# A two-layer trunk with experts: rows fetched and returned by indirect DMA in place of one-hot products, and a conv LayerNorm queued behind the gates

## The chip, the cores and the metric

The kernel runs on one core of a Trainium2 chip. The metric is the device time of one execution in microseconds. Engines are named as in the profile: PE is TensorE (PEld its weight loads), DVE is VectorE, ACT is ScalarE, POOL is GpSimd, SP is SyncE, whose queue issues the transfers of the weights.

## What is computed

256 tokens of 1024 channels go through two layers. Each layer has a mixer (a conv module beside four heads of a gated delta rule, with one output projection) and a feed-forward part, each followed by a LayerNorm. The feed-forward part is dense in layer 0 and in layer 1 a choice of two experts of eight per token. The reference, cut to what the change touches:

```python
def conformer_conv(h_val, h_gate, dw_w, dw_b, ln_g, ln_b):
    h = h_val * jax.nn.sigmoid(h_gate)
    h = causal_depthwise_conv(h, dw_w) + dw_b        # 31 taps, 512 channels
    return jax.nn.silu(layer_norm(h, ln_g, ln_b))

def gated_deltanet(...):
    ...
    o = o * lax.rsqrt(jnp.mean(o * o, -1, keepdims=True) + RMS_EPS) * on_g
    o = o * jax.nn.silu(heads(z))

def hybrid_mixer(...):
    return jnp.concatenate([y_conv, y_dn], axis=-1) @ w_out

def moe_swiglu(x, router_w, w_gate, w_up, w_down):   # 8 experts of width 3584
    top_v, top_i = lax.top_k(x @ router_w, TOP_K)    # TOP_K = 2
    gates = jax.nn.softmax(top_v, axis=-1)
    combine = jnp.sum(jax.nn.one_hot(top_i, N_EXPERTS) * gates[..., None], axis=-2)
    for e in range(N_EXPERTS):
        y = y + combine[..., e:e + 1] * swiglu(x, w_gate[e], w_up[e], w_down[e])
```

## The kernel before

**Stages.** Mixer 0, the dense feed-forward part, mixer 1, the router, the experts and a last LayerNorm run one after the other. All weights come from memory in transfers of 1 MB on SP's queue (`load_w`, L152) into 14 buffers, `raw` and `raw2`.

**Products.** Where fp32 precision is wanted from three fast products, a weight half (128x1024) is split into `whi` (a copy in fp32r on ACT, L160) and `wlo` (the rest, a subtraction on DVE, L161). `prod3` (L205 to L207) then makes three products of them: with whi, with wlo, and whi with the low part of the other operand. Four buffers hold each of whi and wlo.

**Experts.** Each expert takes up to 128 tokens and runs seven steps, one per 512 columns of its width (8 x 7 = 56 steps; experts with more tokens are finished by code behind a branch that is not entered). A step has `gateup` (mg and mu, four loads), the transposes of the hidden values (`turn`, L878) and `down` (md, two loads), which runs one step later and adds to two PSUM banks `y`. The order in the program is gateup of a step, then down of the step before; between the two halves of a gateup comes `turn`.

**In and out of an expert.** `onehot(e)` compares each token's slot number with a row of 0 to 127 (L817): pm is a 256x128 one-hot matrix. `dispatch(e)`, called in step 5 of the expert before, multiplies the tokens xs with pm (16 fp32 products, L850), which gathers and transposes in one; ACT and DVE split the result into the pair `xe` (L853, L854). `combine(e)`, called after the last down of an expert, transposes pm (L823) and casts it (L825), splits y into a pair `ysl` (ACT L829, DVE L830), multiplies back to token rows (eight products, L834) and adds each of four pieces, times the gate of its token (comb), to the sum macc (L835 on DVE).

**Mixers.** The conv's 31 taps are spread: POOL and ACT take 11 or 12 of them, DVE the others (`scalar_tensor_tensor`, L640), in blocks of 128 channels, c = 0 to 3; cv is the sum (L642). The conv's LayerNorm starts with transposes of cv on PE (L650), followed by statistics and scaling on DVE (L653), transposes back (L656), swish on ACT (L657) and a split into the pair yTh, yTl (L659, L660). The delta rule ends with `gate_out(tb, po)` for the two halves of the tokens, tb = 0 and 1 (gate 0 and gate 1 in what follows): squares on ACT (L565), a sum `oss` (L566) and an rsqrt of small steps on DVE (L196 to L201), the gated output o (L571) on DVE, four transposes on PE (L572), and a copy yF (L574). The output projection has products of yF with raw weights (L673) and, after these, `prod3` products with yTh and yTl.

**What sets the order.** Each engine runs its own list of instructions. A scheduler ahead of the program places them, by the data that each needs and by a cost of its own; `tc.issue_after(x)` puts what is issued within it behind the instruction x. So a line's place in the code doesn't tell its place on an engine.

Of the kernel before, what the change touches and what calls it, by code (L numbers as in the profile page):

```python
# [7 lines left out]
F32 = mybir.dt.float32  # L8
# [21 lines left out]
ORDER = (('k', 'log', 'v', 'kk', 'q', 'c0', 'inv', 'c1'), ('k', 'log', 'v', 'kk', 'inv', 'q', 'c0', 'c1'))  # L30
GROUPS = {"c0": (0, 1), "c1": (2, 3), "k": (4, 5), "q": (6, 7), "v": (8, 9)}
# [14 lines left out]
def tile_hybrid_trunk(ctx: ExitStack, tc: tile.TileContext, A: dict, out: bass.AP, stop=None):  # L46
# [259 lines left out]
    def mixer(l):  # L306
        with ExitStack() as late:
# [253 lines left out]
            def gate_out(tb, po):  # L561
                oss = mx.tile([P, NH], F32, name="oss", bufs=2)
                oq = mx.tile([P, NH, P], F32, name="oq", tag="dec", bufs=2)
                for h in range(NH):
                    act.activation(oq[:, h], po[:, h], AF.Square, accum_out=oss[:, h:h + 1])  # L565
                dve.scalar_tensor_tensor(oss, oss, 1.0 / P, ssq[:, tb], op0=OP.mult, op1=OP.add)  # L566
                fac = rsqrt(oss, NH, "4")
                o = mx.tile([P, NH, P], F32, name="o", tag="dec", bufs=2)
                pt = psum.tile([P, NH, P], F32, name="sm")
                for h in range(NH):  # L570
                    dve.scalar_tensor_tensor(o[:, h], po[:, h], fac[:, h:h + 1], zg[:, tb, h], op0=OP.mult, op1=OP.mult)  # L571
                    pe.transpose(pt[:, h], o[:, h], ident)  # L572
                dst = (slice(None), slice(None), slice(tb * P, (tb + 1) * P))
                act.activation(yF[dst], pt, AF.Copy)  # L574

# [38 lines left out]
            gate_out(0, po0)  # L614
# [4 lines left out]
            gate_out(1, po1)  # L619
# [4 lines left out]
            for half in range(2):  # L624
# [10 lines left out]
                for m in range(2):  # L635
                    c = 2 * half + m
                    dve.tensor_scalar(ca[:, m], hp[:, c, 0:T], dwh[:, l, c * CW:c * CW + 1], sm_[:, S_DWB + c:S_DWB + c + 1],
                                      op0=OP.mult, op1=OP.add)
                    for j in range(1, CW - NP):
                        dve.scalar_tensor_tensor(ca[:, m], hp[:, c, j:j + T], dwh[:, l, c * CW + j:c * CW + j + 1], ca[:, m],  # L640
                                                 op0=OP.mult, op1=OP.add)
# [108 lines left out]
    def moe(l):  # L750
        with tc.tile_pool(name="moe", bufs=1) as ex:
# [58 lines left out]

            def onehot(e, base):
                pm = ex.tile([P, 2, P], F32, name="pmx", tag="ysl") if base else ex.tile([P, 2, P], F32, name="pm", bufs=2)
# [7 lines left out]
            def combine(e, pm, py, tag="sm"):  # L820
# [5 lines left out]
                ysl = ex.tile([P, 2, D], F32R, name="ysl")  # L826
                for n in range(2):
                    ns = slice(n * 512, (n + 1) * 512)
                    act.activation(ysl[:, 0, ns], py[n], AF.Copy)  # L829
                    dve.tensor_tensor(ysl[:, 1, ns], py[n], ysl[:, 0, ns].bitcast(F32), op=OP.subtract)  # L830
                    for tb in range(2):
                        pc = psum.tile([P, 512], F32, name=tag)
                        for i in range(2):
                            pe.matmul(pc, pmT[:, tb], ysl[:, i, ns], start=(i == 0), stop=(i == 1))  # L834
# [5 lines left out]
            def dispatch(e):  # L840
                pm = onehot(e, 0) if e else pm0
# [51 lines left out]
            disp, ys = {0: dispatch(0)}, {}  # L893
# [7 lines left out]
            def do_down():  # L901
# [4 lines left out]
                if j == NJ - 1:  # L906
# [150 lines left out]
```

## Time and profile before

| What | Value |
|---|---|
| three runs | 1561.82 to 1564.14 us, median 1562.19 |
| the profiled execution | 1562.18 us, of which its span 1560.4 |
| mean granted clock of PE over the span | 0.989 |
| mixer 0; dense part; mixer 1; router | 0 to 170; 170 to 405; 405 to 528; 528 to 546 us |
| experts; last LayerNorm and output | 546 to 1541; 1541 to 1560.4 us |
| PE busy, experts' stage | 452.99 us of the first 454, 539.54 of the other 541 |
| DVE busy, the same | 413.89 and 477.44 |
| 336 loads of expert weights | 1 MB each |

A page of the profile shows one execution on the core. The views used below are the page itself, a table of stretches (the busy time of each engine in a stretch of the span), groups of like instructions, the chain of waits (followed back from the last instruction, at each step to what released it), the sums of waits by what was waited for, and the timeline of one or all engines. In a row of the timeline the idle time before the instruction, and what ended it, stand in brackets. An operation with `x16` in the program can stand with more pieces in the trace.

### The profile page before, as it was taken

To read this page: it belongs to the slowest core of one execution; us is meant where nothing else is said; L and a number is where in the kernel's file an instruction comes from. 1 tells how busy PE (TensorE), PEld (TensorE's weight loads), DVE (VectorE), ACT (ScalarE), POOL (GpSimd) and SP (SyncE) were. 2 spreads that over 40 slices of the span, in tenths; PEclk is the share of its full clock that TensorE was granted. 3 is DMA by queue.
4 is the path that set the end of the run, shared out by engine and by line. 5 is a ranking of instruction groups with operands and counts; after the bars stand their busy time and mean duration, and the time that the engine had idled before them with its cause. 6 is when DMAs were issued, how large, how long until landed. Compare 5 with 4: busy or idle time off the path is not lost.

```text
span 1560.4 us, 20825 instructions
## 1 busy us (share of the span) xinstructions
PE 1512.6 (97%) x7750; PEld 1254.7 (80%) x7750; DVE 1269.1 (81%) x1775; ACT 991.8 (64%) x1267; POOL 94.1 (6%) x80
## 2 busy tenths in 40 slices
PE   8998999999998999999999999999999999999995
PEld 7884899998885778888888888877887887887884
DVE  5987544447978589899899898889888889889887
ACT  3364244443255288778778777777777777777773
POOL 0252000000144000000000000000000000000000
PEclk9999999999999899999999999999999999999998
DMA  8322555545222789999999989999999999999960
GB/s 354 109 81 101 183 179 186 189 163 189 78 85 85 320 329 377 347 353 368 357 340 375 356 330 367 357 351 339 371 346 344 361 341 339 378 343 331 368 234 29
DMA packets 60731, 430.44 MB, mean 276 GB/s; under 512 B 6736, under 2 KB 7120, under 8 KB 9296
## 3 DMA queue, kind: packets, MB, share of 16 engines
q1 hardware_dynamic: 60624, 429.06, 74.0%
q8 instruction: 62, 1.02, 0.3%
q14 instruction: 45, 0.37, 0.1%
HBM read 427.98 MB, written 1.05 MB: 275 GB/s over the span
## 4 chain that ended last, share of the span: by engine, by line
PE 60%; DVE 4%; issue 1%; ACT 0%; DVEq 0%; ACTq 0%
PE gu L206 13%; PE gu L207 12%; PE gu L205 12%; PE y L206 6%; PE y L207 6%; PE y L205 6%; DVE wlo L161 2%; PE sm L850 2%; PE sm L878 1%; DVE macc L835 1%; PE sm L834 1%; ACT whi L160 0%; DVE lny L249 0%; DVE ln_sto L177 0%; DVE lny L252 0%
## 5 line engine op out<-in xcount | busy, mean ns | idle before, releaser
L161 DVE TENSOR_TENSOR wlo<-raw,whi 128x1024 fp32r<-128x1024 f32 x753 | 889.5, 1221 | 162.1 <-ACT whi L160 148.2
L160 ACT ACTIVATE whi<-raw 128x1024 fp32r<-128x1024 f32 x753 | 775.8, 1057 | 193.7 <-PE gu L207 78.4
L206 PE MATMUL gu<-wlo,xe 128*128 128x512 f32 x892 | 352.9, 396 | 1.9 <-DVE wlo L161 1.3
L205 PE MATMUL gu<-whi,xe 128*128 128x512 f32 x892 | 351.6, 395 | 0.0
L207 PE MATMUL gu<-whi,xe 128*128 128x512 f32 x892 | 348.1, 390 | 0.0
L206 PEld LDWEIGHTS gu<-wlo,xe 128*128 128x128 f32 x892 | 167.6, 188 | 44.1 <-DVE wlo L161 12.3
L205 PEld LDWEIGHTS gu<-whi,xe 128*128 128x128 f32 x892 | 167.5, 188 | 36.5 <-ACT whi L160 1.9
L207 PEld LDWEIGHTS gu<-whi,xe 128*128 128x128 f32 x892 | 167.6, 188 | 33.6
L205 PE MATMUL gu<-xTh,whi 128*128 128x256 f32 x320 | 90.9, 284 | 0.0
L207 PE MATMUL gu<-xTh,wlo 128*128 128x256 f32 x320 | 90.6, 283 | 0.0
L206 PE MATMUL gu<-xTl,whi 128*128 128x256 f32 x320 | 90.5, 283 | 0.0
L640 DVE SCALAR_TENSOR_TENSOR ca<-hp,small,ca 128x256 f32<-128x256 f32 x148 | 72.3, 488 | 3.9
L213 PE MATMUL mm<-xT,raw 128*128 128x256 f32 x240 | 56.8, 390 | 8.4 <-DMA raw<-win 7.0
L206 PEld LDWEIGHTS gu<-xTl,whi 128*128 128x128 f32 x320 | 61.4, 192 | 0.6 <-issue 0.2
L205 PEld LDWEIGHTS gu<-xTh,whi 128*128 128x128 f32 x320 | 61.4, 192 | 0.6 <-issue 0.2
L207 PEld LDWEIGHTS gu<-xTh,wlo 128*128 128x128 f32 x320 | 61.4, 192 | 0.0
L213 PEld LDWEIGHTS mm<-xT,raw 128*128 128x128 f32 x240 | 45.8, 197 | 14.7 <-issue 6.9
L871 ACT ACTIVATE h<-gu 128x512 f32<-128x512 f32 x56 | 33.5, 599 | 37.0 <-PE gu L207 36.8
L634 POOL TENSOR_TENSOR cp<-cp,pr 128x512 f32<-128x512 f32 x42 | 53.6, 1275 | 56.1 <-ACT pr L632 54.2
L632 ACT ACTIVATE pr<-hp,small 128x256 f32<-128x256 f32 x84 | 39.2, 505 | 10.8 <-POOL cp L634 10.8
L872 DVE TENSOR_TENSOR h<-h,gu 128x512 f32<-128x512 f32 x56 | 38.3, 683 | 4.3 <-PE gu L207 3.1
L213 PE MATMUL mm<-xF,raw 128*128 128x256 f32 x176 | 40.5, 380 | 1.2 <-ACT whi L160 1.2
(766 smaller groups left out, 2233.1 us busy)
## 6 DMA issues: line engine op xcount, KB each, us to landing
raw<-mu SPq DMA_DIRECT2D x112, 1024.0 KB, 6.9
raw<-mg SPq DMA_DIRECT2D x112, 1024.0 KB, 6.8
raw<-md SPq DMA_DIRECT2D x112, 1024.0 KB, 6.8
raw<-win SPq DMA_DIRECT2D x23, 1024.0 KB, 5.8
raw<-fgu SPq DMA_DIRECT2D x22, 1024.0 KB, 4.9
raw<-fdn SPq DMA_DIRECT2D x11, 1024.0 KB, 5.0
raw<-wout SPq DMA_DIRECT2D x8, 1024.0 KB, 5.0
xT<-xt SPq DMA_DIRECT2D x2, 512.0 KB, 5.7
```

What stands on the lines that cost most here:

```text
L160: act.activation(hi, src, AF.Copy)
L161: eng.tensor_tensor(low, src, hi.bitcast(F32), op=OP.subtract)
L205: pe.matmul(ps, ah, bh, start=start, stop=False, skip_group_check=True)
L206: pe.matmul(ps, ah, bl, start=False, stop=False, skip_group_check=True)
L207: pe.matmul(ps, al, bh, start=False, stop=stop, skip_group_check=True)
L213: pe.matmul(ps, a, b, start=start, stop=stop, skip_group_check=True)
L632: act.activation(pr[:, m], hp[:, c, j:j + T], AF.Copy, scale=dwh[:, l, c * CW + j:c * CW + j + 1])
L634: pool.tensor_tensor(cp[:, cs], cp[:, cs], pr, op=OP.add)
L640: dve.scalar_tensor_tensor(ca[:, m], hp[:, c, j:j + T], dwh[:, l, c * CW + j:c * CW + j + 1], ca[:, m], op0=OP.mult, op1=OP.add)
L850: pe.matmul(pt[:, k], xs[:, tb, (hf * 4 + k) * P:(hf * 4 + k + 1) * P], pm[:, tb], start=(tb == 0 and k == 0), stop=(tb == 1), skip_group_ ...
L871: act.activation(h, pg, AF.Silu)
L872: dve.tensor_tensor(h, h, pu, op=OP.mult)
```

## The change

**Experts.** Before expert 1 is needed, the tokens xs are written to memory (`xrows`, 256 rows), and `number_rows` makes a list of token numbers and, for each token, the row numbers of its two experts' outputs (that of a row of zeros, where the output is expert 7's). `fetch(e + 1)`, in step 1 of expert e, makes pm as before, multiplies it with the column of token numbers (two products with one column each), casts the result to integers `xi` and has POOL fetch the 128 rows by an indirect DMA (512 KB) into `xg`. `dispatch` transposes xg in eight blocks. `put_away` copies y of experts 0 to 6 to `yst` on ACT and writes it from POOL to the memory `yrows` (512 KB). Expert 7 still has its combine. In its steps 1 to 4 `recall` fetches 128 rows of outputs each, first and second choice of both halves of the tokens, and `collect` adds them to macc, each times its gate, in steps 3 to 6.

**Mixers.** The last 12 of DVE's taps in block c = 3 are held: six behind gate 0's last o, six behind gate 1's. The transposes of cv (L650) wait behind gate 1's last transpose.

```diff
-                    dve.scalar_tensor_tensor(o[:, h], po[:, h], fac[:, h:h + 1], zg[:, tb, h], op0=OP.mult, op1=OP.mult)
-                    pe.transpose(pt[:, h], o[:, h], ident)
+                    d = dve.scalar_tensor_tensor(o[:, h], po[:, h], fac[:, h:h + 1], zg[:, tb, h], op0=OP.mult, op1=OP.mult)
+                    t = pe.transpose(pt[:, h], o[:, h], ident)
...
-            gate_out(0, po0)
+            gated = [gate_out(0, po0)]
...
-            gate_out(1, po1)
+            gated.append(gate_out(1, po1))
...
+                        hold_back = ExitStack()
+                        if c == CT - 1 and j >= CW - NP - 2 * HELD:
+                            hold_back.enter_context(tc.issue_after(gated[j >= CW - NP - HELD][0]))
+                        with hold_back:
+                            dve.scalar_tensor_tensor(ca[:, m], hp[:, c, j:j + T], dwh[:, l, c * CW + j:c * CW + j + 1], ca[:, m],
+                                                     op0=OP.mult, op1=OP.add)
...
-                for c in range(CT):
-                    pe.transpose(pt[:, c], cv[:, c, ts], ident)
+                with tc.issue_after(gated[1][1]):
+                    for c in range(CT):
+                        pe.transpose(pt[:, c], cv[:, c, ts], ident)
...
+            def number_rows():
+                for tb in range(2):
+                    pool.dma_start(xrows[tb * P:(tb + 1) * P], xs[:, tb])
...
+            def fetch(e):
+
+                pm = onehot(e, 0)
+                pi = psum.tile([P, 1], F32, name="sm")
+                for tb in range(2):
+                    pe.matmul(pi, pm[:, tb], tok[:, tb:tb + 1], start=(tb == 0), stop=(tb == 1))
+                xi = ex.tile([P, 1], I32, name="xi", bufs=2)
+                dve.tensor_copy(xi, pi)
+                xg = row4("xg")
+                pool.indirect_dma_start(xg, None, xrows[:, :], bass.IndirectOffsetOnAxis(ap=xi[:, 0:1], axis=0))
+                return pm, xg
+
+            def put_away(e, py):
+                yst = row4("yst")
+                for n in range(2):
+                    act.activation(yst[:, n * 512:(n + 1) * 512], py[n], AF.Copy)
+                pool.dma_start(yrows[e * P:(e + 1) * P], yst)
+
+            def recall(i):
+                yg = row4("yg")
+                pool.indirect_dma_start(yg, None, yrows[:, :], bass.IndirectOffsetOnAxis(ap=yi[:, i % 2, i // 2:i // 2 + 1], axis=0))
+                return yg
+
+            def collect(i):
+                tb, yg = i // 2, recalled[i]
+                dve.scalar_tensor_tensor(acc[:, tb], yg, gt[:, i % 2, tb:tb + 1], acc[:, tb], op0=OP.mult, op1=OP.add)
...
             def dispatch(e):
-                pm = onehot(e, 0) if e else pm0
+                pm, xg = fetched.pop(e) if e else (pm0, None)
...
-                    for tb in range(2) if e else ():
-                        for k in range(4):
-                            pe.matmul(pt[:, k], xs[:, tb, (hf * 4 + k) * P:(hf * 4 + k + 1) * P], pm[:, tb],
-                                      start=(tb == 0 and k == 0), stop=(tb == 1), skip_group_check=True)
+                    for k in range(4) if e else ():
+                        pe.transpose(pt[:, k], xg[:, (hf * 4 + k) * P:(hf * 4 + k + 1) * P], ident)
...
+                if j == NJ - 1 and e < NE - 1:
+                    put_away(e, ys[e])
+                elif j == NJ - 1:
                     combine(e, disp[e][0], ys[e])
...
+                if (e, j) == (0, 1):
+                    number_rows()
+                if j == 1 and e + 1 < NE:
+                    fetched[e + 1] = fetch(e + 1)
+                if e == NE - 1:
+                    if j > 2:
+                        collect(j - 3)
+                    if 1 <= j <= 4:
+                        recalled.append(recall(j - 1))
```

Where the scheduler puts this on the engines, by the order of the two programs:

PE, the dispatch for expert 5 within a step of expert 4. `sm` is a PSUM tile, gu and y the products of gateup and down. Before, the first of its five pieces:

```order
L205 MATMUL gu<-whi,xe 128x512
L850 MATMUL sm<-pm,xs 128x128 x3
L206 MATMUL gu<-wlo,xe 128x512
L207 MATMUL gu<-whi,xe 128x512
L205 MATMUL gu<-whi,xe 128x512
```

After (line numbers are those of the changed file):

```order
L206 MATMUL gu<-whi,xe 128x512
L923 MATMUL sm<-keep,xg 128x128 x6
L207 MATMUL gu<-wlo,xe 128x512
L208 MATMUL gu<-whi,xe 128x512
L206 MATMUL gu<-whi,xe 128x512
```

The 16 products, in pieces of 3, 2, 3, 2 and 6, become eight transposes, in pieces of 6 and 2.

DVE, in the combine of expert 5, before:

```order
L161 TENSOR_TENSOR wlo<-raw_11199,whi 128x1024
L161 TENSOR_TENSOR wlo<-raw_11221,whi 128x1024 x2
L161 TENSOR_TENSOR wlo<-raw_11271,whi 128x1024 x2
L830 TENSOR_TENSOR ysl<-y,ysl 128x512 x2
L835 SCALAR_TENSOR_TENSOR macc<-sm,comb,macc 128x512 x2
L161 TENSOR_TENSOR wlo<-raw,whi 128x1024
L835 SCALAR_TENSOR_TENSOR macc<-sm,comb,macc 128x512 x2
L161 TENSOR_TENSOR wlo<-raw,whi 128x1024 x2
L882 TENSOR_TENSOR hp__11320<-sm,hp__11320 128x512
```

After, DVE has nothing of an expert's output until expert 7; there the four additions stand among the splits like this (yg are the rows fetched back):

```order
L162 TENSOR_TENSOR wlo<-raw,whi 128x1024 x4
L883 SCALAR_TENSOR_TENSOR macc<-yg,gt,macc 128x1024
L162 TENSOR_TENSOR wlo<-raw,whi 128x1024 x2
L883 SCALAR_TENSOR_TENSOR macc<-yg,gt,macc 128x1024
L162 TENSOR_TENSOR wlo<-raw,whi 128x1024
L944 TENSOR_TENSOR h<-h,gu 128x512
L162 TENSOR_TENSOR wlo<-raw,whi 128x1024 x3
L954 TENSOR_TENSOR hp__12407<-sm,hp__12407 128x512
L162 TENSOR_TENSOR wlo<-raw,whi 128x1024 x2
L883 SCALAR_TENSOR_TENSOR macc<-yg,gt,macc 128x1024
L162 TENSOR_TENSOR wlo<-raw,whi 128x1024 x2
L883 SCALAR_TENSOR_TENSOR macc<-yg,gt,macc 128x1024
```

Two output splits and four additions in a row per expert have gone; four additions of twice the width stand in two of expert 7's steps.

DVE, gate 0 in mixer 0, before (rs are the steps of rsqrt):

```order
L199 TENSOR_TENSOR rs_t_987<-rs_y_986 128x4
L640 SCALAR_TENSOR_TENSOR ca<-hp,small,ca 128x256
L200 SCALAR_TENSOR_TENSOR rs_t_987<-rs_t_987,oss 128x4
L640 SCALAR_TENSOR_TENSOR ca<-hp,small,ca 128x256
L201 SCALAR_TENSOR_TENSOR rs_y_986<-rs_t_987,rs_y_986 128x4
L642 TENSOR_TENSOR cv<-ca,cp 128x512
L199 TENSOR_TENSOR rs_t_987<-rs_y_986 128x4
L200 SCALAR_TENSOR_TENSOR rs_t_987<-rs_t_987,oss 128x4
L201 SCALAR_TENSOR_TENSOR rs_y_986<-rs_t_987,rs_y_986 128x4
L571 SCALAR_TENSOR_TENSOR o<-sm,rs_y_986,zg 128x128 x4
```

After:

```order
L200 TENSOR_TENSOR rs_t_987<-rs_y_986 128x4
L201 SCALAR_TENSOR_TENSOR rs_t_987<-rs_t_987,oss 128x4
L202 SCALAR_TENSOR_TENSOR rs_y_986<-rs_t_987,rs_y_986 128x4
L572 SCALAR_TENSOR_TENSOR o<-sm,rs_y_986,zg 128x128 x4
L647 SCALAR_TENSOR_TENSOR ca<-hp,small,ca 128x256 x5
L567 SCALAR_TENSOR_TENSOR oss<-oss,ssq 128x4
L647 SCALAR_TENSOR_TENSOR ca<-hp,small,ca 128x256
L197 TENSOR_SCALAR rs_t_1027<-oss 128x4
L198 TENSOR_SCALAR rs_y_1026<-rs_t_1027 128x4
```

The taps (L640, now L647) no longer alternate with the small steps ahead of o; cv and the LayerNorm's statistics, which followed at once, have gone behind gate 1.

## Rows read from the trace of the kernel before

**Rows 1.** The page, busy time: us, share of the span, instructions of each engine.

```profile
PE 1512.6 (97%) x7750; PEld 1254.7 (80%) x7750; DVE 1269.1 (81%) x1775; ACT 991.8 (64%) x1267; POOL 94.1 (6%) x80
```

**Rows 2.** Stretches: length, busy PE, PEld, DVE, ACT, POOL (count), PEclk, DMA share, GB/s.

```profile
1100.00:1200.00 100.00, 99.68 (x460) 80.64 (x459) 90.04 (x90) 75.11 (x83) 0.00 (x0) 1.00 0.94 349
```

**Rows 3.** Groups, 560 to 1560.4 us: what xcount | busy us, mean ns | idle before.

```profile
L161 DVE TENSOR_TENSOR wlo<-raw,whi 128x1024 fp32r<-128x1024 f32 x663 | 779.9, 1220 | 66.1 <-ACT whi L160 52.2
...
L835 DVE SCALAR_TENSOR_TENSOR macc<-sm,comb,macc 128x512 f32<-128x512 f32 x32 | 22.5, 745 | 3.6 <-PE sm L834 3.6
...
L830 DVE TENSOR_TENSOR ysl<-y,ysl 128x512 fp32r<-128x512 f32 x16 | 10.2, 680 | 2.2 <-ACT ysl L829 2.2
```

**Rows 4.** Chain of waits, whole run: start us, length us, engine and line.

```profile
682.30 0.56 PE sm L834 x2
...
761.47 3.57 PE sm L850 x32
775.94 0.44 PE sm L878 x4
792.73 0.44 PE sm L878 x4
805.69 0.57 PE sm L834 x2
...
1053.41 0.52 PE sm L834 x2
...
1430.35 0.52 PE sm L834 x2
```

**Rows 5.** Chain of waits, 1165 to 1192 us, round the combine of expert 4.

```profile
1171.67 1.18 DVE wlo L161
...
1181.71 0.74 DVE macc L835
```

**Rows 6.** Waits of PEld, 560 to 1500 us: total us, times, longest us.

```profile
PEld gu L206 <- DVE wlo L161: 10.9, 36, 0.5
```

**Rows 7.** Waits of SyncE's queue, the same stretch.

```profile
SPq L152 <- DVE wlo L161: 806.2, 315, 7.1
```

**Rows 8.** Timeline of PE in the router: start us, us, instructions, shapes, count.

```profile
529.44 1.95 PE L767 MATMUL sm<-rwt,xTf 128*128 128x8 f32 x16
```

**Rows 9.** The page, DMA issues: transfers, KB each, median us to landing.

```profile
raw<-mu SPq DMA_DIRECT2D x112, 1024.0 KB, 6.9
```

**Rows 10.** Timeline of 113 to 131 us, GpSimd and VectorE; idle before in brackets.

```profile
113.93 9.45 POOL L634 TENSOR_TENSOR cp<-cp,pr 128x512 f32<-128x512 f32 x7 [0.38 <-ACT pr L632]
...
122.56 1.90 DVE L161 TENSOR_TENSOR wlo<-raw,whi 128x1024 fp32r<-128x1024 f32 x1 [1.91 <-ACT whi L160]
```

**Rows 11.** Timeline of 128 to 160 us, the end of mixer 0.

```profile
128.07 3.63 DVE L640 SCALAR_TENSOR_TENSOR ca<-hp,small,ca 128x256 f32<-128x256 f32 x7
...
128.96 0.22 ACT L565 ACTIVATION_READ_ACCUMULATOR oq<-sm 128x1 f32 x1
...
136.75 0.69 PE L650 MATMUL ca<-keep,cv 128*128 128x128 f32 x2 [6.81 <-DVE cv L642]
...
137.27 1.13 DVE L571 SCALAR_TENSOR_TENSOR o<-sm,rs_y,zg 128x128 f32<-128x128 f32 x4
...
153.86 0.69 DVE L660 TENSOR_TENSOR yTl<-cv,yTh 128x512 fp32r<-128x512 f32 x1 [3.67 <-ACT yTh L659]
...
158.97 0.80 PE L205 MATMUL mm<-whi,yTh 128*128 128x512 f32 x1
```

**Rows 12.** Timeline of 476 to 530 us, the same place of mixer 1.

```profile
482.10 7.84 DVE L640 SCALAR_TENSOR_TENSOR ca<-hp,small,ca 128x256 f32<-128x256 f32 x15
...
495.31 0.33 PE L572 MATMUL sm<-keep,o 128*128 128x128 f32 x1 [1.98 <-DVE o L571]
```

**Rows 13.** Stretches of 5 us, columns as in rows 2.

```profile
505.00:510.00 5.00, 5.00 (x17) 2.31 (x17) 1.43 (x3) 2.67 (x6) 0.00 (x0) 1.00 0.69 241
...
515.00:520.00 5.00, 5.00 (x20) 3.40 (x19) 1.66 (x3) 0.00 (x0) 0.00 (x0) 1.00 1.01 428
```

More of the change, by code (lines that the diff above doesn't have):

```diff
@@ L570, in gate_out @@
                 for h in range(NH):
[L571 to L572 removed]
+                    d = dve.scalar_tensor_tensor(o[:, h], po[:, h], fac[:, h:h + 1], zg[:, tb, h], op0=OP.mult, op1=OP.mult)
+                    t = pe.transpose(pt[:, h], o[:, h], ident)
                 dst = (slice(None), slice(None), slice(tb * P, (tb + 1) * P))
                 act.activation(yF[dst], pt, AF.Copy)
+                return d.ins, t.ins
             u = mx.tile([P, 2, NH, P], F32, name="u", tag="Dm")
@@ L809, in moe, with row4 @@
             acc = ex.tile([P, 2, D], F32, name="macc")
+            rows = ctx.enter_context(tc.tile_pool(name="rows", bufs=1, space=bass.MemoryType.DRAM))
+            xrows = rows.tile([T, D], F32, name="xrows")
+            yrows = rows.tile([(NE - 1) * P + 1, D], F32, name="yrows")
+            LAST = (NE - 1) * P
+            tok = ex.tile([P, 2], F32, name="tok")
+            yi = ex.tile([P, 2, 2], I32, name="yi")
+            def row4(name, dt=F32, shape=(P, D)):
+                return ex.tile(list(shape), dt, name=name, tag="row4", bufs=2)
@@ new lines, in number_rows @@
+            def number_rows():
+                for tb in range(2):
+                    pool.dma_start(xrows[tb * P:(tb + 1) * P], xs[:, tb])
+                zero = row4("zero")
+                pool.memset(zero[0:1], 0.0)
+                pool.dma_start(yrows[LAST:LAST + 1], zero[0:1])
+                pt = psum.tile([P, 1], F32, name="sm")
+                pe.matmul(pt, striu, ones[:, 0:1], start=True, stop=True)
+                dve.tensor_copy(tok[:, 0:1], pt)
+                dve.tensor_scalar(tok[:, 1:2], tok[:, 0:1], float(P), None, op0=OP.add)
+                n = NE - 1
+                er = ex.tile([P, NE], F32, name="er")
+                pr = ex.tile([P, 2, NE], F32, name="pr")
+                ok = ex.tile([P, 2, NE], F32, name="ok")
+                yf = ex.tile([P, 2, 2], F32, name="yf")
+                dve.tensor_scalar(er, iota[:, 0:NE], float(P), float(-LAST), op0=OP.mult, op1=OP.add)
+                dve.tensor_scalar(ok, posm, float(P) - 0.5, None, op0=OP.is_lt)
+                for tb in range(2):
+                    dve.tensor_tensor(pr[:, tb], posm[:, tb], er, op=OP.add)
+                dve.tensor_tensor(pr, pr, ok, op=OP.mult)
+                for j in range(2):
+                    dve.tensor_tensor(ok, sel2[:, j], pr, op=OP.mult)
+                    dve.tensor_reduce(yf[:, j], ok[:, :, 0:n], axis=mybir.AxisListType.X, op=OP.add)
+                dve.tensor_scalar(yf, yf, float(LAST), None, op0=OP.add)
+                dve.tensor_copy(yi, yf)
@@ new lines, in fetch @@
+            def fetch(e):
+                pm = onehot(e, 0)
+                pi = psum.tile([P, 1], F32, name="sm")
+                for tb in range(2):
+                    pe.matmul(pi, pm[:, tb], tok[:, tb:tb + 1], start=(tb == 0), stop=(tb == 1))
[4 more added lines that the diff above has]
+                return pm, xg
@@ L833, in combine @@
                         for i in range(2):
-                            pe.matmul(pc, pmT[:, tb], ysl[:, i, ns], start=(i == 0), stop=(i == 1))
+                            pe.matmul(pc, pmT[:, tb], ysl[:, i], start=(i == 0), stop=(i == 1))
                         dve.scalar_tensor_tensor(acc[:, tb, ns], pc, comb[:, tb, e:e + 1], acc[:, tb, ns], op0=OP.mult, op1=OP.add)
@@ L892, in moe @@
             steps = [(e, j) for e in range(NE) for j in range(NJ)]
-            disp, ys = {0: dispatch(0)}, {}
+            fetched, recalled, ys = {}, [], {}
+            disp = {0: dispatch(0)}
             gates()
```

12 lines of the change are left out of this document (5 added, 7 removed).

## Prediction

> **What bounds the kernel now.** I read the stretches first: the table of stretches has TensorE busy 99.68 us of 100 between 1100 and 1200 us, at granted clock 1.00, VectorE 90.04, ScalarE 75.11, GpSimd nothing, and 349 GB/s come in [rows 2]; over the whole span TensorE has 97% [rows 1]. So the experts' stage (546 to 1541 us) lasts as long as TensorE's list of products, and VectorE is the next engine, with a tenth in hand.
>
> The chain of waits then shows what a period of one expert consists of [rows 4]. Seven plain steps are 16.79 us each (from the transposes at 775.94 to those at 792.73), 117.53. The dispatch (16 products of L850 that the trace counts as 32 passes) takes 3.57 us, and the combine's products follow the last step. From 682.30 to 805.69 one period is 123.4 us. From 1053.41 to 1430.35 three periods are 376.9, that is 125.65 each: later experts lose over 2 us more although they do the same work.
>
> The chain of one late combine shows where that is lost [rows 5]: splits of weights (wlo) and additions to macc on VectorE stand in a chain that elsewhere holds products alone. VectorE is asked for four additions and two output splits while it must also split weights. The waits agree: TensorE's weight loads wait for wlo 36 times, 10.9 us, while SyncE's load queue waits 806.2 us for buffers and no engine is seen waiting for a weight transfer [rows 6, 7].
>
> **Dispatch.** L850's 32 passes of 3.57 us go for experts 1 to 7; eight transposes take their place, one pass each. Transposes cost 0.11 us a pass (x4 in 0.44 [rows 4]), so 0.88. The gain is 2.69 us x 7 = **-18.8**, all of it on the path, as PE never idles there.
>
> **Combine.** For experts 0 to 6 the eight products of L834 go. In the chain they stand as four pairs, the first 0.56 [rows 4], the three others 0.46, 0.47 and 0.46, together 1.95. The two transposes of the one-hot (estimated at 0.22 by the passes above) go too: 2.17 x 7 = **-15.2**. What is added there are two copies on ScalarE in place of two it did before, and a GpSimd DMA.
>
> **Fetch.** TensorE gets two one-column fp32 products, four passes, per expert. The router's products with 8 columns ran 16 passes in 1.95, so 0.122 each [rows 8]: 0.49 x 7, and 0.25 once for numbering the tokens, **+3.7**.
>
> **Lost time at late combines.** Six periods from 682.30 to 1430.35 are 748.05; at 117.53 + 3.57 + 2.17 = 123.27 they would be 739.6, so 8.4 us is lost. After the change VectorE has neither macc's four additions (745 ns) nor the two output splits (680 ns) at that place [rows 3], and per expert it drops from about 111 busy us (0.90 x 123.4) by 4 x 0.745 + 2 x 0.68 + 0.42 (the cast of the transposed one-hot, estimated) to 106.3, while TensorE's period becomes 117.53 + 0.88 + 0.49 = 118.9. Its share stays at 0.89, so the general slack is not larger; it is the lump that goes. I take **-6**, between 0 and -8.4.
>
> **Collection.** Expert 7's steps get four additions of 128x1024. By two of 745 ns each is 1.5, 6 in all; two stand in one step, two in the next. A step leaves VectorE 16.79 x 0.10 = 1.7 us, so each pair overdraws by 1.3 and the slack of neighbouring steps takes most of it. The rows gathered must have landed: write, then read, each at most as long as the median weight transfer of 6.9 us [rows 9], 13.8 after step 0, while the first addition stands behind step 3. **+1**, from 0 to +8 (the four in full, and another wait of 2).
>
> **GpSimd beside VectorE.** The only row of the two together: a weight split of 1.90 us while GpSimd's seven products (113.93 to 123.38) still ran, against a mean of 1.22 [rows 3, 10]. So an overlap can cost 0.7. Fourteen fetches and stores and four recalls at 0.7 are 12.6, against VectorE's slack of a tenth: **+1**, from 0 to +10. How long GpSimd works on an indirect transfer no row shows.
>
> By the Trainium skill, "SBUF — State Buffer", Who interferes with whom, a VectorE instruction with two SBUF inputs, as every weight split is, contends with a GpSimd instruction that reads SBUF, and whoever comes first locks the other out. The row of 1.90 agrees in direction; that descriptor work does it, no run here shows.
>
> **Mixer 0.** ScalarE has gate 0's squares at 129.18, but VectorE's chain of rsqrt stands between convolution taps (one tap to one small step), and the transposes wait for the last conv block until 136.75, 6.81 us idle; gate 0's own transposes come behind them [rows 11]. With 12 taps held (0.52 each by 7 in 3.63) and cv (0.7) gone from there, 6.9 of the 9.2 us between 128.07 and the gate's output at 137.27 go; the small steps then wait on one another, and I estimate that this gives 1.4 back: the output starts at 131.8, 5.5 earlier. Gate 1 then comes as much earlier. But the conv LayerNorm now begins behind gate 1: its two chains of statistics, transposes and swish took from 136.75 to 153.86 interleaved with the gates. Behind gate 1 at about 140, six taps (3.1) and cv (0.7), they start at 144 and need some 11, end 155, where the yTh products started at 158.97. So 4 of the 5.5 arrive: **-4**, from 0 (LayerNorm ends at 159) to -7 (the whole idle time).
>
> **Mixer 1.** There the transposes' last wait is 1.98, for o [rows 12]. VectorE's taps end at 489.9, when ScalarE has only just read the gate's product; with 12 held VectorE idles there, up to 12 x 0.52 = 6.2, and does them later, ahead of LayerNorm. Gain and loss nearly cancel: **-0.5**, from -3 (the 1.98 and one us of the small steps) to +2 (a third of the idle time is missed later).
>
> **Kept at nothing:** tokens written to memory at the start of the stage (1 MB, two DMAs), needed only for expert 1's transposes four steps later; index arithmetic on VectorE, some 15 small operations in expert 0's steps, covered by the tenth. Without that cover it would be about 3. The one read of the count that stands earlier on SyncE's queue has its value long before.
>
> **The sum** is -18.8 - 15.2 + 3.7 - 6 + 1 + 1 - 4 - 0.5 = -38.8. The profiled execution took 1562.18 (span 1560.4), at the median of the runs, 1562.19. That gives **1523.4**, with TensorE's terms alone at 1531.9.
>
> **Rivals.** (A) *The waits stay.* VectorE at 0.89 keeps making TensorE late and the mixers return nothing: 1562.2 - 30.3 + 0 to 9 = 1532 to 1541. For it: VectorE's share does not fall. Against: early experts at the same share lose nothing [rows 4].
>
> (B) *Transfers become the bound.* A step takes six loads, 6.29 x 10^6 bytes, in 16.79 us: 375 GB/s, and an expert's seven steps with 0.52 in and 0.52 out are (44.04 + 1.05)/118.9 = 379. If the 349 of a full stretch [rows 2] were the limit, 336 loads (352.3) and 7.3 of rows would take 360/0.349 = 1031 us from 505, where the rate rises [rows 13], ending at 1536, with the rest of a step (5) and the tail (1541 to 1560) 1560: no gain; a limit of 360 would leave 1530. Against it: 428 GB/s ran in 515 to 520 [rows 13], and the load queue waits for buffers, not the reverse [rows 7].
>
> The Trainium skill, "DMA: Bandwidth & Descriptors", Specifications, gives about 358 GB/s as one core's part of the memory, by which the same sum would end at an estimated 1536; the row of 428 contradicts it as a limit for a core alone.
>
> (C) *GpSimd shuts VectorE out, slower.* It decides from where VectorE's 106.3 per expert plus two transfers' preparation exceed the old mean period of 124.7 (748.05/6) plus the 0.6 that the mixers return per expert: (125.3 - 106.3)/2 = 9.5 us of full exclusion per GpSimd DMA. At 12, each period is 130.3, 5.6 x 7 - 4.5 = +35: 1597. For it: 1.90 against 1.22. Against: even in that row GpSimd's work only stretched one split by half.
>
> (D) *Gathered tokens arrive late.* Fetched in step 1, transposed in step 5: 67 us, against 6.9 [rows 9]. It would need ten times the slowest median; no price taken. If the gather did need 74, 7 x 7 = 49 would turn the gain into +10.
>
> **How the numbers follow.** Forecast (1511 to 1531) 0.62; A 0.20; B 0.07, 0.03 of it within 3 us of before; C 0.08; D and the rest, slower, 0.03. Two tenths of a per cent, 3 us, is about what a measurement of this kernel tells from no change. Faster: 0.62 + 0.20 + 0.04 = 0.86; same 0.03; slower 0.11. The range of 8 in 10 takes the forecast and A: 1511 (the sum with -8.4, -7, -3 and no additions, 1514, and 3 for what is left out) to 1541.
>
> **What would show it.** In the trace after: chain pieces of 0.11 per transpose in dispatch; L834 only once; a period of 119 us in all experts, late ones too (A: 120 to 121.5, with wlo in the chain; C: wlo means well over 1.22; B: ScalarE or VectorE waiting for a DMA, SyncE's waits for buffers gone); o of gate 0 in mixer 0 at about 132; yTh products at about 155. I am wrong if the period stays above 121.5, or if a wait for xg or yg stands in TensorE's or VectorE's list.

## The result, and the profile after

The changed kernel takes 1545.49 us (median, 1543.67 to 1546.49), the kernel before 1563.09 on the same chip: a ratio of 0.9888, interval 0.9876 to 0.9900. That is 17.6 us faster, the way that was forecast but less than half of the 38.8, and above the stated range. Of the two signs that the prediction named for being wrong, one came: a wait for yg stands in VectorE's list (the periods ahead of expert 7 stayed under 121.5). The two profiled spans, 1560.4 and 1543.1, differ by 17.3, so the traces can stand for the times.

First the place. The experts' first product with wlo starts at 551.98 us, against 551.02 before: all that lies ahead of the experts together has become 1.0 us longer, where 4.5 less was forecast. The last product of expert 7's down starts at 1522.23, against 1539.95. So the experts' stage is 18.7 us shorter, where 34.3 was forecast.

```profile
1539.95 0.39 PE L207 MATMUL y<-whi,hp__13215 128*128 128x512 f32 x1
```

```profile
1522.23 0.39 PE L208 MATMUL y<-whi,hp__13096 128*128 128x512 f32 x1
```

(The first line is of the kernel before, the second of the kernel after.)

The stretches of the kernel after, columns as in [rows 2]:

```profile
1100.00:1200.00 100.00, 99.73 (x455) 80.84 (x454) 88.33 (x85) 78.63 (x87) 2.54 (x2) 1.00 0.99 378
1360.00:1460.00 100.00, 89.44 (x386) 71.07 (x385) 80.53 (x75) 67.37 (x74) 5.87 (x5) 0.95 0.92 345
```

The first row answers [rows 2]: PE is as full as before, and more is done in the time (378 GB/s against 349, so transfers were no bound; SyncE's queue still waits 786.9 us for buffers, as in [rows 7]). The second is new: PE misses 10.6 us of 100, in expert 7. The chain of waits of the whole run, and what leads to the hole:

```profile
639.77 0.87 PE sm L923 x8
...
758.71 0.87 PE sm L923 x8
770.49 0.44 PE sm L950 x4
787.28 0.44 PE sm L950 x4
...
988.23 0.66 PE sm L923 x6
...
1108.75 0.66 PE sm L923 x6
...
1402.82 7.51 DMA yrows<-yst
...
1411.07 5.93 DMA yg<-yrows,yi
```

Dispatch is 0.87 for eight transposes, as the prediction had it (0.88), and the first period, 639.77 to 758.71, is 118.94 (118.9). From the third expert on a period is 120.5 (988.23 to 1108.75). At the end the chain goes through memory: expert 6's output is written in 7.51 us and the first rows are fetched in 5.93. The timeline there shows who stands behind it:

```profile
1403.50 4.63 DVE L162 TENSOR_TENSOR wlo<-raw,whi 128x1024 fp32r<-128x1024 f32 x4 [0.20 <-ACT whi L161]
...
1417.03 1.28 DVE L883 SCALAR_TENSOR_TENSOR macc<-yg,gt,macc 128x1024 f32<-128x1024 f32 x1 [8.90 <-DMA yg<-yrows,yi]
```

```profile
1419.51 0.80 PE L207 MATMUL gu<-wlo,xe 128*128 128x512 f32 x1 [9.01 <-DVE wlo L162]
```

DVE reaches the first addition at 1408.1, waits for its rows, and holds all weight splits behind it until 1417.0; PE then waits 9.01 us for a wlo.

The duration of each step of an expert, from one set of transposes of h to the next in the trace, is the measure for the rest (kernel after, us; experts are counted from 0; step 1 contains the fetch, step 5 the dispatch; where the transposes change place, as in expert 2, single steps mean nothing and are left out):

```
          step 1    2      3      4      5      6      0 of next   sum
expert 1  17.29  16.79  16.79  16.79  17.69  16.79  16.79        118.93
expert 4  17.92  16.86  16.90  16.86  18.22  16.86  16.86        120.48
expert 7  29.40  18.32  17.47  16.86  16.87  16.86
```

Expert 7 loses 29.40 + 18.32 + 17.47 - 3 x 16.87 = 14.6 us. In the groups, answering [rows 3]:

```profile
L162 DVE TENSOR_TENSOR wlo<-raw,whi 128x1024 fp32r<-128x1024 f32 x670 | 784.5, 1220 | 93.5 <-ACT whi L161 85.3
...
L883 DVE SCALAR_TENSOR_TENSOR macc<-yg,gt,macc 128x1024 f32<-128x1024 f32 x4 | 5.1, 1280 | 8.9 <-DMA yg<-yrows,yi 8.9
```

A split takes 1220 ns as before, though GpSimd now prepares 18 transfers beside them, and the single splits that ran beside such a preparation took 1.21 to 1.23 us: GpSimd shuts nobody out here.

### The profile page after: what moved, and what is told of

Its sections match the earlier page's. It is cut to its first block, busy times and chain, and to the rows that moved or that the text cites. A ratio compares the mean times of both kernels' runs of the same rounds, so it can differ in the third digit from the quotient of the medians.

```text
span 1543.1 us, 20424 instructions
## 1 busy us (share of the span) xinstructions
PE 1486.6 (96%) x7542; PEld 1228.9 (80%) x7542; DVE 1245.5 (81%) x1750; ACT 983.7 (64%) x1267; POOL 117.2 (8%) x102
## 4 chain that ended last, share of the span: by engine, by line
PE 52%; issue 8%; DVE 2%; DMA 1%; ACT 1%; POOL 0%; DVEq 0%; ACTq 0%; POOLq 0%
PE gu L207 11%; PE gu L208 11%; PE gu L206 11%; PE y L206 6%; PE y L207 6%; PE y L208 6%; PE sm L950 1%; DVE wlo L162 1%; ACT whi L161 1%; DMA yrows<-yst 0%; DMA yg<-yrows,yi 0%; PE sm L923 0%; DVE lny L250 0%; DVE ln_sto L178 0%; DVE macc L909 0%
## 5 line engine op out<-in xcount | busy, mean ns | idle before, releaser
L647 DVE SCALAR_TENSOR_TENSOR ca<-hp,small,ca 128x256 f32<-128x256 f32 x148 | 72.3, 488 | 4.1
L867 POOL DMA_INDIRECT xg<-xrows,xi x7 | 11.0, 1575 | 526.7 <-DVE xi L865 526.7
L361 ACT ACTIVATE scacc<-mm,small 128x256 f32<-128x256 f32 x24 | 11.4, 473 | 47.8 <-DVE scacc L363 27.4
## 6 DMA issues: line engine op xcount, KB each, us to landing
yrows<-yst POOLq DMA_DIRECT2D x7, 512.0 KB, 10.2
```

What stands on the lines that cost most here:

```text
L361: act.activation(acc[:, m], pp[:, m], AF.Copy, scale=w[:, 3:4])
```

## Experiments

All ratios are against the kernel before, on the same chip.

### The two halves of the change apart

**e1**, the mixers' part in the kernel before:

> The kernel before with the mixers' part of the change alone (12 taps held, the conv LayerNorm's transposes behind gate 1); experts as before. Theory M (the mixers' part gives nothing, since LayerNorm behind gate 1 and a longer stretch at half clock in the router take back what gate 0 gains): within 2 us of the kernel before, 1561 to 1565 us. Rival (the mixers' part is worth the 4.5 us of the prediction, and the experts' start one us later comes from writing the tokens to memory): 1557 to 1559 us, first product with wlo of the experts near 546.

**e2**, the experts' part alone:

```diff
-HELD = 6
+HELD = 0
...
-                with tc.issue_after(gated[1][1]):
-                    for c in range(CT):
-                        pe.transpose(pt[:, c], cv[:, c, ts], ident)
+                for c in range(CT):
+                    pe.transpose(pt[:, c], cv[:, c, ts], ident)
```

> The changed kernel with the mixers as they were before (no tap held, no wait for gate 1). Theory M: the same time as the changed kernel, 1543 to 1547 us, and the experts' stage as long as there (989.2 us before, some 970.5 now). Rival: the mixers' part is worth 4.5 us, 1549 to 1551 us.

e1 took 1564.53 us, 1.0010 (1.0001 to 1.0019); e2 1544.60, 0.9891 (0.9876 to 0.9906), as the whole change. Theory M holds: the mixers' part gives nothing, and by e1's interval (0.2 to 3.0 us longer) it rather costs something. The trace of the changed kernel shows where its gain goes. Mixer 0, answering [rows 11]:

```profile
127.14 3.55 POOL L611 TENSOR_TENSOR zg<-zg,ong 128x512 f32<-128x512 f32 x2 [3.57 <-ACT zg L610]
...
129.69 1.01 DVE L567 SCALAR_TENSOR_TENSOR oss<-oss,ssq 128x4 f32<-128x4 f32 x1
...
133.00 1.13 DVE L572 SCALAR_TENSOR_TENSOR o<-sm,rs_y,zg 128x128 f32<-128x128 f32 x4
...
156.01 0.30 PE L664 MATMUL ca<-keep,xn 128*128 128x128 f32 x1 [1.11 <-DVE xn L661]
...
156.10 0.50 PE L206 MATMUL mm<-whi,yTh 128*128 128x512 f32 x1
```

Gate 0's output starts at 133.00 (131.8 forecast, 137.27 before), and the yTh products at 156.10 (155 forecast, 158.97 before). The mixer's last product starts 2.4 us earlier than before, 167.65 against 170.06. In mixer 1 the same order, answering [rows 12]:

```profile
511.19 0.33 PE L664 MATMUL ca<-keep,xn 128*128 128x128 f32 x1 [0.87 <-ACT cv L665]
512.73 0.50 PE L206 MATMUL mm<-whi,yTh 128*128 128x512 f32 x1 [1.21 <-ACT yTh L667]
...
513.41 0.63 PE L206 MATMUL mm<-whi,yTh 128*128 128x512 f32 x1
```

The yTh products start 3.7 us earlier than before (516.39), but PE has waited for LayerNorm (0.87 and 1.21), and several run at 0.63 us instead of 0.39; the last starts at 526.62, only 0.85 earlier. The first of them in the kernel before:

```profile
516.39 0.80 PE L205 MATMUL mm<-whi,yTh 128*128 128x512 f32 x1
```

Stretches there, after, columns as in [rows 2]:

```profile
510.00:513.00 3.00, 0.92 (x4) 0.44 (x4) 2.96 (x9) 2.23 (x4) 0.00 (x0) 1.00 1.00 423
513.00:517.00 4.00, 4.00 (x13) 3.08 (x12) 2.26 (x7) 0.00 (x0) 0.00 (x0) 0.57 1.01 426
```

PE was busy 0.92 of 3 us, and after it the granted clock is 0.57 for 4 us, mostly the lower of its two levels (1.2 GHz); before the change it stayed at 1.00 from 510 to 517. Then the router: granted clock 0.56 in 528 to 546 against 0.72 before, and its last 16 products take 3.76 us against 2.03. A stretch and a row of PE's timeline from the kernel before, then the same from the one after:

```profile
528.00:546.00 18.00, 15.45 (x90) 14.59 (x90) 10.72 (x51) 3.29 (x6) 0.00 (x0) 0.72 0.53 208
...
544.22 2.03 PE L786 MATMUL gu<-pm,xs 128*128 128x128 f32 x16
```

```profile
528.00:546.00 18.00, 15.68 (x79) 15.02 (x78) 10.20 (x58) 2.63 (x5) 0.93 (x2) 0.56 0.49 176
...
543.53 3.76 PE L794 MATMUL gu<-pm,xs 128*128 128x128 f32 x16
```

So mixer 0 gives 2.4, mixer 1 returns 1.5 of it, and the router 1.8. All traces of this document, those of the runs below too, sorted by their mixers (one execution each), bear this out:

| Mixers | Traces | Experts' first product with wlo, us | Granted clock, 528 to 546 |
|---|---|---|---|
| as before | before, e2, e7, e10, e13 | 550.10 to 552.01 | 0.72 in all |
| both changed | after, e1, e3, e4, e5, e6, e11 | 550.82 to 552.61 | 0.54 to 0.64 |
| mixer 0 alone changed | e8, e9, e12 | 548.35 to 549.58 | 0.62, 0.72, 0.72 |

The start scatters by 2 us among kernels with the same mixers, so the +1.0 alone would show little; that mixer 0 alone starts the experts earlier than either, the groups show. The router's lower clock comes with the changed mixer 1, in seven traces of seven (without it in one of eight, e8). How it follows stays open: in e11 mixer 1 itself ran at 1.00 from 505 to 528, and the router still at 0.54.

### Expert 7's additions

**e3**, the additions one per step where the code calls them:

```diff
-                dve.tensor_tensor(h, h, pu, op=OP.mult)
+                hold['h'] = dve.tensor_tensor(h, h, pu, op=OP.mult)
...
-                        collect(j - 3)
+                        with tc.issue_after(hold['h'].ins):
+                            collect(j - 3)
```

> The changed kernel with each of the four additions of fetched rows (collect) issued behind h of expert 7's steps 3, 4, 5 and 6, one per step, where the change's code calls them. In the changed kernel they stand two steps earlier on VectorE and the first waits 8.90 us for its rows. Theory C (that wait, with the splits queued behind it, is what expert 7 loses: its steps 1 to 3 take 29.40, 18.32 and 17.47 us against 16.87): 12 to 15 us faster than the changed kernel, 1530 to 1534 us, no wait of VectorE for yg. Rival (the additions cost VectorE's time wherever they stand, 5.1 us and their knock-on): 1540 to 1545 us, the loss spread over four steps.

1535.23 us, 0.9824 (0.9811 to 0.9838): 10 us less than the changed kernel, with no wait for yg. The first two additions:

```profile
1447.50 1.28 DVE L883 SCALAR_TENSOR_TENSOR macc<-yg,gt,macc 128x1024 f32<-128x1024 f32 x1
...
1465.41 1.28 DVE L883 SCALAR_TENSOR_TENSOR macc<-yg,gt,macc 128x1024 f32<-128x1024 f32 x1
```

Theory C holds, but with 2 us less than expected. The steps with an addition take 17.92, 17.94 and 17.93 us against 16.87: an operation of 1.28 us still costs 1.05. And expert 7's step 1 takes 17.80 without any addition, so 0.9 of its 14.6 us was not theirs.

**e4**, in addition the cast of the token numbers behind h of step 1:

```diff
-                dve.tensor_copy(xi, pi)
+                with tc.issue_after(hold['h'].ins):
+                    dve.tensor_copy(xi, pi)
```

> The kernel of e3 with the cast of the token numbers (xi) also moved on VectorE, behind h of step 1 of each expert, so that VectorE doesn't wait 0.68 us for the two small products ahead of it. In late experts of the changed kernel the step with the fetch takes 17.9 us, in the first two 17.29. Theory X (that wait in VectorE's list is the 0.6): 2 to 4 us faster than e3, that step at 17.3 to 17.4. Rival (the 0.6 is the order of the late experts in general, as their plain steps of 16.87 against 16.79): the same as e3 within 1 us.

1535.59 us, 0.9831 (0.9818 to 0.9844): no gain; the step with the fetch stays at 17.8 and a wait of VectorE for the same two products, now in front of the next one-hot, takes the old one's place (1.4 us in two, between 560 and 1500 us). Theory X falls. Nor is the fetch as such what lengthens that step in late experts: expert 7 fetches no tokens and has its 17.80 too.

### The late experts

In e3's trace an early and a late step differ in what stands ahead of h. Timeline of the second expert and of the fifth, ScalarE and VectorE:

```profile
704.31 1.06 ACT L161 ACTIVATE whi<-raw 128x1024 fp32r<-128x1024 f32 x1 [0.28 <-PE gu L208]
...
705.67 0.60 ACT L943 ACTIVATE h<-gu 128x512 f32<-128x512 f32 x1 [0.30 <-PE gu L208]
```

```profile
1066.16 0.60 ACT L943 ACTIVATE h<-gu 128x512 f32<-128x512 f32 x1 [1.66 <-PE gu L208]
...
1067.74 1.23 DVE L162 TENSOR_TENSOR wlo<-raw,whi 128x1024 fp32r<-128x1024 f32 x1 [1.96 <-ACT whi L161]
```

Late, h comes to ScalarE before PE has the gate product and holds the splits behind it 1.66 us; VectorE then waits 1.96. The transposes of h follow at 1070.52, within down and ahead of the next gateup, where early ones stand in the middle of that gateup (719.06 in the kernel after). Six runs moved single operations of this (e8 beside them returned to the mixers).

**e5**, **e6**: h behind the first, or the second, whi of the following down. The edit takes h out of gateup (the cut is of e5; e6 has 1 for the 0):

```diff
+                        if nxt and kh * 2 + kk == 0:
+                            with tc.issue_after(hold['whi'].ins):
+                                h = swish(*nxt)
```

> The kernel of e3 with h (the swish of the gate product, on ScalarE) issued behind the first whi of the following down in every step. In the late experts of e3 h stands ahead of the four whi of down and waits 1.66 us for TensorE each step, and VectorE then 1.96 us for the next whi; in the first two experts one or more whi stand ahead of h and the wait is 0.30. Theory H (this order on ScalarE takes VectorE's slack in the late experts, so that each extra operation there costs its whole length): late experts go back to the pace of the first two, plain steps 16.87 to 16.79, step 1 17.9 to 17.3, step 5 18.2 to 17.7, the steps with an addition 17.92 to about 16.9; 1.5 us x 5 + 3 = 10 faster than e3, 1524 to 1527 us. Rival P (VectorE is short of time whatever the order, its 90% being the limit): within 2 us of e3, 1533 to 1537 us.

> As e5 with h behind the second whi of the following down. Theory H: as e5 or up to 2 us slower, since h and the transposes behind it come a split (1.06 us) later. Rival P: as e3, 1533 to 1537 us.

1536.89 us, 0.9834 (0.9820 to 0.9847), and 1547.34, 0.9903 (0.9888 to 0.9918). Theory H falls as stated; e5 lies where rival P had it, e6 some 10 us above. In e5 h no longer waits on ScalarE, but its second half does on VectorE:

```profile
1070.17 0.69 DVE L947 TENSOR_TENSOR h<-h,gu 128x512 f32<-128x512 f32 x1 [1.83 <-PE gu L208]
```

**e7**: e5's edit in the kernel before.

> The kernel before with the same order of h, nothing else changed. Theory H: the loss of its late experts (periods of 125.7 us against 123.4) is the same order and not the combine's lump of VectorE work; the periods fall to 123.4 to 124 us and the time by 6 to 9 us, to 1553 to 1556 us. Rival L (the prediction's reading: four additions and two splits in a row make the late loss): at most 1 us a period comes back, 1557 to 1562 us.

1563.19 us, 1.0004 (0.9995 to 1.0013): nothing, as rival L and the fate of e5 would both have it.

**e8**: e5 with the mixers' part in mixer 0 only.

```diff
-                        if c == CT - 1 and j >= CW - NP - 2 * HELD:
+                        if l == 0 and c == CT - 1 and j >= CW - NP - 2 * HELD:
...
+                if l == 0:
+                    behind.enter_context(tc.issue_after(gated[1][1]))
```

> The kernel of e5 with the mixers' part of the change in mixer 0 alone, mixer 1 as before. In the trace of e1 mixer 0 ends 3.1 us earlier, mixer 1 only 0.2 earlier, and the router takes 1.3 us longer at a lower clock. Theory N (mixer 1 and the router behind it lose what mixer 0 gains): 3 to 4.5 us faster than e5, with the yTh products of mixer 1 and the router as in the kernel before. Rival (the 3 us of mixer 0 are lost in the dense part, where weights come late): within 1 us of e5.

1534.03 us, 0.9816 (0.9802 to 0.9829), 2.9 less than e5 on the same chip: theory N, just under its range of 3 to 4.5. Mixer 1's last product starts at 525.54 there, 1.1 us earlier than in the changed kernel.

**e9**, **e10**, **e11**: the transposes of h behind the first half of the next gateup, in e8, in the kernel of e7, and in e3.

```diff
+                with tc.issue_after(hold['mm'].ins):
                     for k in range(4):
                         pe.transpose(pt[:, k], h[:, k * P:(k + 1) * P], ident)
```

> The kernel of e8 with the transposes of h (turn) issued on TensorE behind the last product of the first half of the next gateup, where the code calls them; e8 keeps h behind one whi of down. In the late experts of e3 and e5 these transposes stand ahead of that gateup, 1.4 us behind h on VectorE, so h and the split behind the transposes make VectorE or ScalarE wait in turn (1.96 us for whi in e3, 1.83 us for TensorE in e5). Theory T (h and turn close together are the late experts' loss; apart, as in the first two experts, neither waits): late experts at 118.9 to 119.3 us a period and additions at nearly no cost, 1.5 us x 5 + 2.5 = 10 faster than e8, 1523 to 1526 us. Rival P (VectorE's work of 90% is the limit): within 2 us of e8, 1532 to 1536 us.

> The kernel before with both orders of e9 (h behind one whi of down, turn behind the first half of the next gateup). Theory T: the late experts' loss in the kernel before is this order too, periods go from 125.7 to 123.4 to 124 us, 1553 to 1556 us. Rival L (the combine's lump on VectorE): about 1 us a period remains lost, 1557 to 1562 us.

> The kernel of e3 with the turn of e9 alone, h left to the scheduler, mixers as in the changed kernel. Theory T: the late experts gain as in e9 if the scheduler puts h behind a whi of down by itself; if h stays ahead of all four, it waits for TensorE as in e3 and 1526 to 1530 us result. Rival P: 1533 to 1537 us, as e3.

1552.69 us, 0.9933 (0.9919 to 0.9946); 1572.98, 1.0064 (1.0050 to 1.0077); 1556.10, 0.9955 (0.9942 to 0.9969). All slower than what they started from: theory T falls in this form, and rival P too, since it expected no difference. Late plain steps are 17.5 us. Now the copy of the transposes (hp) stands too early on ScalarE:

```profile
1012.75 0.60 ACT L960 ACTIVATE hp__8826<-sm 128x512 fp32r<-128x512 f32 x1 [2.10 <-PE sm L957]
```

Each edit had left the other operations to the scheduler, which put one of them ahead of what PE had ready.

**e12**: the whole order of the first two experts written out for all, with e3's additions and e8's mixers; **e13**: that order in the kernel before. The copy of the transposes goes behind the last whi of gateup, its low half behind the last wlo, the transposes where e9 had them (not in the cut):

```diff
+                with tc.issue_after(hold['whi'].ins):
+                    act.activation(hh, pt, AF.Copy)
+                with tc.issue_after(hold['wlo'].ins):
+                    dve.tensor_tensor(hl, pt, hh.bitcast(F32), op=OP.subtract)
...
+                        if nxt and kh * 2 + kk == 0:
+                            with tc.issue_after(hold['whi'].ins):
+                                h = swish(nxt[0])
+                        if nxt and kh * 2 + kk == 2:
+                            with tc.issue_after(hold['wlo'].ins):
+                                times(h, nxt[1])
```

> The kernel of e8's parts (additions behind h of steps 3 to 6, the mixers' part in mixer 0 alone) with the order of the first two experts written out for all: ScalarE has eight whi of gateup, the pair hp of the step before, one whi of down, h, three whi; VectorE eight wlo, its half of hp, three wlo, its half of h, one wlo; the transposes stand behind the first half of gateup's products. In e5 and e9 one of these places was moved and another wait came in its stead (VectorE 1.83 us for TensorE, ScalarE 2.10 us). Theory O (the late experts lose by such a wait in each step, which the order of the first two does not have): all experts at 118.9 us a period, steps with an addition at about 17, 1522 to 1526 us. Rival S (the late experts are slower whatever the order, since weights, VectorE's share or GpSimd's transfers set the pace there): 120 us or more a period, 1531 to 1537 us.

> The kernel before with the order of e12 in its experts, nothing else changed. Theory O: periods of 123.4 to 123.8 us in all experts, 1553 to 1556 us; then the late loss before the change was order and not the combine's work on VectorE. Rival L (the combine's four additions and two splits in a row on VectorE are the loss): late periods stay at 125 us or more, 1560 to 1564 us.

1524.96 us, 0.9761 (0.9748 to 0.9774), and 1559.35, 0.9973 (0.9962 to 0.9984). The steps:

```
                  step 1    2      3      4      5      6      0 of next   sum
e12, expert 4     17.29  16.79  16.79  16.79  18.30  16.79  17.07        119.82
e12, expert 7     16.79  16.79  16.79  16.79  16.79
e13, expert 4     16.56  16.79  16.79  16.79  20.39  16.79  20.50        124.59
before, expert 1  16.79  16.79  16.79  16.79  20.38  16.79  19.05        123.40
before, expert 4                                                         125.68
```

In e12 plain steps of late experts are 16.79 to the hundredth, the fetch costs 0.50 as in the first two, and the four additions in expert 7's steps 3 to 6 cost nothing. Theory O holds in these; the period, 119.82, is 0.9 above the 118.9 of its expectation, left in the steps with the dispatch and the output's copies. One late step of e12:

```profile
1058.59 0.58 ACT L966 ACTIVATE hp__9321<-sm 128x512 fp32r<-128x512 f32 x1
1059.45 1.06 ACT L161 ACTIVATE whi<-raw 128x1024 fp32r<-128x1024 f32 x1 [0.28 <-PE gu L208]
...
1060.81 0.60 ACT L949 ACTIVATE h<-gu 128x512 f32<-128x512 f32 x1 [0.30 <-PE gu L208]
```

And the stretch in which the changed kernel had its hole:

```profile
1360.00:1460.00 100.00, 100.00 (x452) 82.16 (x451) 92.79 (x86) 81.10 (x85) 11.23 (x4) 1.00 0.99 392
```

PE is full with VectorE at 92.79 and 392 GB/s: neither VectorE's share nor the transfers were the limit of the late experts. In e13 the late period falls from 125.68 to 124.59; 1.1 us of the late loss before was order, and 1.2 stays, nearly all in the step with the combine (20.50 against 19.05). So theory O has half of it. That the other half is rival L's work on VectorE is not shown: the first experts have the same work there and take 19.05, and e13 left the combine's own operations to the scheduler. A late combine of e13 waits on ScalarE ahead of the copy of y and on VectorE ahead of macc, an early one does not:

```profile
1177.17 1.09 ACT L829 ACTIVATE ysl<-y 128x512 fp32r<-128x512 f32 x2 [1.20 <-PE y L207]
...
1179.99 1.41 DVE L835 SCALAR_TENSOR_TENSOR macc<-sm,comb,macc 128x512 f32<-128x512 f32 x2 [0.90 <-PE sm L834]
```

```profile
804.93 1.07 ACT L829 ACTIVATE ysl<-y 128x512 fp32r<-128x512 f32 x2
...
807.96 1.41 DVE L835 SCALAR_TENSOR_TENSOR macc<-sm,comb,macc 128x512 f32<-128x512 f32 x2
```

## Why the prediction was wrong

**Right.** Dispatch (0.87 measured for 0.88), the combine and the fetch: the first period fell from 123.40 to 118.93, by 4.47, where the terms give 2.69 + 2.17 - 0.49 = 4.37. These terms, -30.3 in all, arrived. No rival among B, C and D came: more GB/s than before, splits of 1220 ns, xg in time.

**Collection** is the step that failed: "the first addition stands behind step 3". That is its place in the code; on VectorE the scheduler had put the first pair into the step after step 0 of expert 7 and the second pair into the next. The order printed ahead of the prediction shows the two pairs; to which step they belong had to be followed there, and was taken from the code. The other half of that step was right: write and read through memory took 7.51 + 5.93 us, under the bound of 13.8. With the addition two steps early that is 8.9 us of waiting for VectorE and 14.6 for the expert (13.7 without the 0.9 that e3 leaves in step 1), instead of 1. e3 gave 10 us back by the place alone.

**VectorE's slack.** The prediction counted a tenth of each step as room for an extra operation. In the late experts this idle time was the waits behind h, [0.30] early and [1.66] and [1.96] late, and an addition of 1.28 cost 1.05 (e3). With the order mended it cost nothing at a higher share of busy time (e12). Idle time that an engine spends behind a wait in its own list is no room for what is queued behind that wait.

**Lost time at late combines**, -6, failed too. By difference this and GpSimd (+1) came to about -3 (-18.7 + 30.3 - 14.6), but that is a remainder and no measurement. Over the six periods that the prediction counted, nothing came back: 7.7 us were lost before (748.05 against 6 x 123.40), and 8.1 are lost in e3, which has no hole in expert 7 (from 691.27 to 1412.95, the first down products of experts 1 and 7: 721.68 against 6 x 118.93). The combine went from that place, and the loss stayed: after the change a late period costs 1.5 more than an early one (120.48 against 118.93), and from the third expert on where it was from the fourth. e13 shows that in the kernel before 1.1 of 2.3 us a period were order already; the cause of the other 1.2 stays open. Rival A expected late periods of 120 to 121.5, as measured, and gave VectorE's share as the cause; e12 shows that after the change the cause is the order.

**Mixers**, -4.5 forecast, +1.0 measured. Mixer 0's mechanism was right and its term too large (2.4 instead of 4): gate 0's chain took longer by 1.2 us (0.85 of it in one small step that now ran beside a product of GpSimd, 1.01 us instead of 0.16), and LayerNorm behind gate 1 ends 1 us later than assumed. Mixer 1 came as +1.5 for -0.5, within its range (to +2), since PE runs dry ahead of the yTh products. The router at a lower clock (1.8) was missing: of it nothing was said.

Of the 21.2 between 38.8 and 17.6, 13.6 stand in expert 7's first steps and 5.5 ahead of the experts, both measured. The 2 that are left are what the late experts and GpSimd fell short by; as a remainder they close the sum and test nothing. e12 comes to the predicted time (1524.96 and 1523.4) only with three repairs that the change doesn't have, so it is no support for the forecast.

## What to carry to other kernels

Where a scheduler sets the order, read the place of a new operation from the order and not from the code, above all of one that waits for a transfer: everything queued behind it on its engine waits as well. Before you count idle time as room, see what ends it; if it is a wait in the engine's own list, an added operation can cost nearly its length (1.05 of 1.28 us here). And when moving one operation mends a wait, look for the next one that moves up into it: in the late experts single moves gave nothing or lost 10 to 21 us, and the complete order gave 9.

## What the runs showed of the hardware

- A 128x4 operation of VectorE with two inputs in SBUF took 1.01 us instead of 0.16 while GpSimd's product of 128x512 ran, and ended with it (129.69 + 1.01 = 130.70, and 127.14 + 3.55 = 130.69). The Trainium skill, "SBUF — State Buffer", Who interferes with whom, says that such a pair contends and the later one is shut out; this row agrees. Eighteen DMAs prepared by GpSimd left the mean split at 1220 ns, and the splits beside them at 1.21 to 1.23 us: in these traces that preparation shut VectorE out of nothing.
- Reading rows by an index took no longer than a plain transfer of the same size from GpSimd: 512 KB in 9.6 us (median of xg) beside 10.2 for the plain write of yst, both beside the stream of weights, of which 1 MB took 7.3; GpSimd is busy 1.0 to 2.0 us for a fetch.
- 2.1 us of waits of PE in mixer 1 were followed by 4 us at a granted clock of 0.57, and the router ran at 0.56 instead of 0.72. With mixer 1 changed the router ran at 0.54 to 0.64 in seven traces, without at 0.72 in seven of eight: a change of order in one stage was paid in a later one.
